# A hybrid decoder block: a bank of its own for retention's state, weight differences kept between two stages, and eight pages for the x sums

## The chip, the core and the metric

The kernel runs on one core of a Trainium2 chip. The metric is the device time of one execution in microseconds, lower is better. The core's engines are TensorE (PE in the profile, its weight loads PEld), VectorE (DVE), ScalarE (ACT), GpSimd (POOL) and SyncE (SP), whose queue issues nearly all DMAs of the part that this case is about. Each engine takes its instructions in the order in which the program gives them to it. Matmuls write to PSUM, which the kernel uses as eight banks, each 128 partitions x 512 fp32.

## The reference

One decoder layer on x of 1024 tokens x 1024 channels, in float32:

```
h    = rms_norm(x)
P    = h @ w_in                       # retention q, k, v, gate: 4 x 512; attention: the rest
ret  = retention, 8 heads of 64 channels, chunks of 128 tokens:
         inner = (q k^T) * decay mask
         o     = inner @ v + (q * decay) @ state
         state = state * decay + (k * decay)^T @ v
ret  = rms_norm per head(ret) * silu(gate)
dif  = differential attention, 4 heads (two softmax maps per head)
x    = x + concat(ret, dif) @ w_out
x    = x + (silu(h2 @ w_gate) * (h2 @ w_up)) @ w_down,   h2 = rms_norm(x), 2816 wide
```

## The kernel before

**Products.** Every fp32 operand is split into a high part and the rest, both fp32r, and a term of a matrix product is three matmuls (high x high, rest x high, high x rest). The input projection of retention's columns is made by seven products in the place of eight (Strassen's way), once for each half p of the columns: p = 0 runs P2, P4, P6, P7, P5, P3 (its P1 and half of P2 stand beside the last attention units, in `lead`), p = 1 runs P1, P2, P6, P5, P3, P7, P4. A product is four tiles j = 0 to 3 of 128 tokens x 512 columns; a tile adds four inner blocks k into one bank, so it is 4 x 3 = 12 matmuls. It needs its weights, four pages of 128x512 (k = 0 to 3) that `prepare` makes out of blocks of w_in and splits (`halves_`: ACT writes the high part `whi`, DVE the rest `wlo`), and its x block. For P6, P7, P5 and P3 this is a sum of blocks of the normalised x that was written to memory earlier (`sumd`): `x_sum` loads one page, ACT casts the high part and DVE subtracts the rest. The pages for these loads are the two `raw` pages, in turn.

**P6, P4 of the first half.** Four weight blocks a, b, d, c of each k go into P4, P6, P5, P3 and P7. Beside the last attention units (steps ND to ND + 2 of the first loop) `t4_load`, `t4_minus`, `t4_scale` and `t4_sum` load them, make the differences a - b and d - c, and of these the weights of P4 into pages named `spare` (and `pr[8]`); the table `EARLY` says which pages. P6 of p = 0 then loads a, b and c of each k again, subtracts a - b again, and makes its weights of that; P5, P3 and P7 use the a and c pages of P6.

**Retention.** A unit (p, t) is a group p of four heads and a chunk t of 128 tokens, t in order. Its steps: load and rotate q and k (DVE); turn, four transposes on PE, copied out of the bank by ACT; inner, q k^T into bank 6; DVE multiplies by the mask into `iT`; state, (k)^T v into columns 256 to 511 of bank 7, which DVE adds to the running state `rg`, GpSimd scaling it; out, iT v and q state into columns 0 to 255 of bank 7; ACT copies it out and squares it, DVE reduces, GpSimd takes the reciprocal root, ACT scales, DVE multiplies by the gate. `mix_turn(t)` transposes what the units of chunk t left and splits it for `o_proj`, the product with w_out; `norm` transposes its result for the FFN. The transposes of the units go through bank 3, those of `mix_turn` and `norm` through banks 1 and 2.

**Order.** From the second product stage on to the first FFN products, each step is a job with an engine, an estimated duration, and keys that it reads and writes (`add`). `Plan` sets one time for every job: products have goals in their order, other jobs a latest time worked back from these, and a list schedule with the estimated durations gives the order on every engine; PE's own order is made this way too. A key stands for a buffer: two jobs are ordered only where a key is shared. The two halves of bank 7 have keys of their own, `b7o` (out) and `b7u` (state).

In the rows below, `h`, `m` and `pp` are PSUM tiles; `h_4014` is bank 6, `h_4015` bank 7, `m_4011` bank 3, `pp_3703` and `m_4010` banks 1 and 2. `wx` and `wy` are the two big pages that hold retention's small tiles (rotated q and k, iT, v, gates, state), `rowa_89` to `rowa_96` the pages `mixd[0]` to `mixd[7]`, `spare_3700` the eight spare pages, `cd` the memory that holds partial sums.

Of the kernel before, what the change touches and what calls it, by code (L numbers as in the profile page):

```python
# [107 lines left out]
def block_kernel(ctx: ExitStack, tc: tile.TileContext, x, norm1_g, w_in, ret_norm_g, dq_g, dk_g,  # L108
# [508 lines left out]
    def t4_load(k, which=range(4)):  # L617
        early[k] = [spare[at] for at in EARLY[k]]
        for n in which:
            SY.dma_start(early[k][n].rearrange("p (a b) -> p a b", b=256), win_block(0, n % 2, n // 2 * 4 + k))  # L620
# [8 lines left out]
    def t4_sum(k):  # L629
        a, b, d, c = early[k]  # L630
        V.scalar_tensor_tensor(out=d, in0=d, scalar=g1col[:, 4 + k:5 + k], in1=b, op0=ALU.mult, op1=ALU.subtract)

    EARLY = [(0, 1, 2, 3), (4, 5, 6, 7), (0, 1, 3, 4), (5, 7, 8, 4)]
    LEAD = {ND: [(4, snap, 0), (1, t4_load, 0), (2, t4_load, 1), (5, t4_minus, 0, 0), (7, t4_minus, 0, 1)],
            ND + 1: [(0, snap, 1), (4, c11, 0), (0, t4_scale, 0), (1, t4_minus, 1, 0), (2, t4_sum, 0), (3, t4_load, 2, range(3)),
                     (4, t4_minus, 1, 1), (5, t4_scale, 1), (6, t4_sum, 1),
                     (6, t4_load, 2, (3,)), (7, t4_load, 3, range(3))],
            ND + 2: [(0, c11, 1), (4, snap, 2), (0, t4_minus, 2, 0), (1, t4_minus, 2, 1), (2, t4_load, 3, (3,)),
                     (2, t4_scale, 2), (3, t4_minus, 3, 0), (4, t4_sum, 2), (5, t4_scale, 3), (6, t4_minus, 3, 1),
# [6 lines left out]
    for s in range(ND + 3):  # L646
        if s == ND:
            difw.close()
            prp = ctx.enter_context(tc.tile_pool(name="prp", bufs=9, side="right"))
            pr = [prp.tile([P, 512], F32, tag="pr", name="pr") for _ in range(9)]  # L650
            late["spare"] = act.tile([P, 8 * 512], F32, tag="act", name="spare")
            spare += [late["spare"][:, i * 512:(i + 1) * 512] for i in range(8)] + [pr[8]]
            small = prp.tile([P, 48], F32, name="small", bufs=1)
            lead_bank += [bankp(), bankp()]
            main = lead()
            order["pinned"] = True
            r_tables()
            order["pinned"] = False
# [23 lines left out]
    sx = ctx.enter_context(tc.tile_pool(name="sx", bufs=3))  # L682
    sxt = [sx.tile([P, 4, 2, 4, P], F32R, tag="sx", name="sx") for _ in range(3)]
    sbs = ExitStack()
# [109 lines left out]
    def dma(to, src, r=(), w=(), **kw):  # L794
        return add("SP", 0.8, lambda: SY.dma_start(to, src), r, w, lag=2.8, **kw)

# [30 lines left out]

    spare = [(f"R{i}", page) for i, page in enumerate(spare[:8])]
    prk = [(f"pr{i}", pr[i]) for i in range(9)]
    rowk = [(f"ra{i}", mixd[i]) for i in range(NT)]  # L830
    rawk = [(f"raw{i}", wp.tile([P, 512], F32, tag="raw", name="raw", bufs=NRAW)) for i in range(2)]
    held = [spare[2], spare[6], spare[3], prk[8]]
    wraw = Ring(rowk[4:8] + [prk[8]])
    keep_r = Ring([spare[i] for i in (0, 4, 5, 7, 1, 2, 6, 3)])
    sraw = Ring(rawk)
# [25 lines left out]
    def prepare(p, name, k, n):  # L861
# [4 lines left out]
        elif name == "P6":  # L866
            a, c = keep_r(), keep_r()
            held_w[k] = a, c
            (ka, a), (kc, c) = a, c
            load_raw(ka, a, p, 0, 0, k)  # L870
            kb, b = rawload(p, 0, 1, k)
            load_raw(kc, c, p, 1, 1, k)
            tt(a, a, b, ALU.subtract, [ka, kb], [ka])
            act_copy(b, a, [ka], [kb], ga)
# [26 lines left out]
    def x_sum(name, j):  # L901
        key, page = sraw()
        dma(page, sumd[SUM_OF[name], j], (), [key])
        hi, lo = (BLOCK[name][:, j, i].rearrange("p k e -> p (k e)") for i in range(2))
        act_copy(hi, page, [key], [f"x{name}{j}h"])
        tt(lo, page, hi.bitcast(F32), ALU.subtract, [key, f"x{name}{j}h"], [f"x{name}{j}l"])

# [100 lines left out]
    ca_r, cb_r = Ring(rowk[0:2]), Ring(rowk[2:4])  # L1008
    turn_bank, side_bank = Ring([3]), Ring([1, 2])
    WS = ["rc", "rn", "sqr", "onr", "qkr0", "qkr1", "qkr2", "qbd0", "qbd1", "vh0", "vh1", "gs0", "gs1",  # L1010
# [6 lines left out]
    def unit(p, t, due=None):  # L1017
# [45 lines left out]
        if t + 1 < NT:  # L1063
            def state():
                for a in range(2):
                    T.matmul(bank[7][:, 256 + a * P:256 + (a + 1) * P], qkr[:, 256 + a * P:256 + (a + 1) * P],
                             vh[:, a * P:(a + 1) * P], start=True, stop=True)
            add("PE", 0.46, state, [qk, vk], ["b7u"])
            gg = cs[:, C_G128 + 2 * p:C_G128 + 2 * p + 2].unsqueeze(2)
            up = bank[7][:, 256:512].rearrange("p (a e) -> p a e", e=P)  # L1070
            o_, n_ = (x_[1].rearrange("p (a e) -> p a e", e=P) for x_ in (old, new))
            for hd in range(2):
                h = halves[hd]
                if t > 0:
                    tt(n_[h, :, h], up[h, :, h], o_[h, :, h], ALU.add, ["b7u", old[0]], [new[0]], dur=0.3)
                else:
                    tt(n_[h, :, h], up[h, :, h], gg[h].broadcast_to([HD, 2, HD]), ALU.mult, ["b7u"], [new[0]], dur=0.3)
            if t > 0:
                tt(n_, n_, gg.broadcast_to([P, 2, P]), ALU.mult, [new[0]], [new[0]], "POOL", 1.1)

        def out_():
            for a in range(2):
# [3 lines left out]
                for hd in range(2):  # L1086
                    T.matmul(o[:, hd * HD:(hd + 1) * HD], iT[:, (2 * a + hd) * P:(2 * a + hd + 1) * P],
                             vh[:, a * P + hd * HD:a * P + (hd + 1) * HD], start=t == 0, stop=t == 0 or hd == 1)
        add("PE", 1.37 if t else 0.92, out_, [tk, ik, vk] + ([old[0]] if t else []), ["b7o"])
        stay = p == 0 and t < 4  # L1090
        mk, m_ = onr if stay else prk[4 + t % 4]
        ob = m_ if stay else m_[:, 256 * p:256 * p + 256]
        add("ACT", 0.28, lambda: A.copy(ob, bank[7][:, 0:256]), ["b7o"], [mk])
        sq4 = sqr[1].rearrange("p (g d) -> p g d", d=HD)
# [64 lines left out]
    def mix_turn(t):  # L1159
        key, page = px[t][1]  # L1160
        dma(page, mixdd[t], (), [key])
        for q, (key, page) in enumerate((prk[4 + t % 4], px[t][1])):
            b = side_bank()

            def go(b=b, page=page):
                for j in range(4):
                    T.transpose(bank[b][:, j * P:(j + 1) * P], page[:, j * P:(j + 1) * P], ident)
            add("PE", 0.36, go, [key], [f"b{b}"])
            n = 2 * (t % 2) + q
            hi, lo = slot[n]  # L1170
            act_copy(hi, bank[b], [f"b{b}"], [f"wh{n}"], dur=0.48)
            tt(lo, bank[b], hi.bitcast(F32), ALU.subtract, [f"b{b}", f"wh{n}"], [f"wl{n}"])
# [41 lines left out]
    def norm(t):  # L1214
# [11 lines left out]
        for q in (t // 4, 1 - t // 4):  # L1226
# [362 lines left out]
```

## Time and profile before

| | |
|---|---|
| median of 3 runs | 1200.89 us (1200.55 to 1201.44) |
| the profiled execution | 1201.5 us, of which the span of instructions is 1199.7 us |
| granted clock of TensorE | 1.00 |
| busy: PE, DVE, ACT, POOL | 1182.1, 911.8, 607.1, 528.4 us |

The stages by the trace, in us from the start of the span:

| stretch | what runs | PE busy |
|---|---|---|
| 0 to 273.10 | attention, its projection, P1 and P2 of p = 0 | 265.72 of 273.10 |
| 273.10 to 332.22 | P4, P6, P7, P5, P3 of p = 0 | 57.29 of 59.12 |
| 332.22 to 436 | the seven products of p = 1, first units | 103.78 of 103.78 |
| 436 to 486 | o_proj, most units | 46.47 of 50.00 |
| 486 to 571 | o_proj, norm | 85.00 of 85.00 |
| 571 to 600 | first FFN products | 28.17 of 29.00 |
| 600 to 1199 | FFN | 595.70 of 599.00 |

A row of the trace gives the start in us, the length in us, the engine, line and operation with out<-in, and in brackets how long the engine was idle just before and what released it. All operations are recorded by one helper, so their line is L136 everywhere. A matmul on fp32 operands (retention's) counts as two. A row of waits gives what waited <- what it waited for: us in total, times, the longest. A row of groups gives a kind of instruction, xcount, then busy us, mean ns | idle time before them and its releasers. A row of the chain (the work that ended last, followed back) has start, length and what ran.

### The profile page before, as it was taken

The numbers are of one execution on the slowest core, as the hardware profiler recorded it, in microseconds if no ns is written. First come the engines' busy times: TensorE is split into PE (matmuls) and PEld (weight loads), VectorE is DVE, ScalarE is ACT, GpSimd is POOL, SyncE is SP. The second block draws the span as 40 slices with busy tenths as digits, with TensorE's granted clock in tenths as the row PEclk, the third lists the DMA queues.
The fourth block names the chain that finished last, engine by engine and source line by source line (L and its number), as shares of the span: only waits on it lengthen the run. The fifth ranks groups of instructions, "written<-read, shape, count | busy, mean of one in ns | idle before, by whom it ended". The sixth has DMA issues, their size and how long they took to land.

```text
span 1199.7 us, 17494 instructions
## 1 busy us (share of the span) xinstructions
PE 1182.1 (99%) x5872; PEld 1000.7 (83%) x5872; DVE 911.8 (76%) x1533; ACT 607.1 (51%) x1332; POOL 528.4 (44%) x611
## 2 busy tenths in 40 slices
PE   8999999999999999999999999999999999999998
PEld 6898989887788887888888888888888888888887
DVE  6987888887878978547988666666666659798696
ACT  6865666656365758635544434343443434444442
POOL 2678787630001214211077545654466536164053
PEclk9999999999999999999999999999999999999999
DMA  7267676358844754222233233323234277933341
GB/s 207 67 138 144 97 137 105 80 185 263 292 150 152 254 170 141 90 78 71 89 114 124 96 100 111 115 98 96 93 109 132 74 266 266 377 106 97 97 128 73
DMA packets 120984, 167.42 MB, mean 140 GB/s; under 512 B 12096, under 2 KB 65472, under 8 KB 120768
## 3 DMA queue, kind: packets, MB, share of 16 engines
q1 hardware_dynamic: 113952, 155.76, 40.1%
q0 software_dynamic: 5760, 10.49, 6.7%
q8 instruction: 46, 0.75, 0.3%
q14 instruction: 42, 0.34, 0.1%
q10 hardware_dynamic: 1184, 0.07, 0.1%
HBM read 114.12 MB, written 54.26 MB: 140 GB/s over the span
## 4 chain that ended last, share of the span: by engine, by line
PE 89%; DVE 5%; DMA 3%; ACT 2%; issue 1%; POOL 0%; SPq 0%; DVEq 0%; ACTq 0%
PE h L136 39%; PE pp L136 29%; PE m L136 19%; PE big L136 3%; DMA raw<-sumd 1%; DVE wlo L136 1%; DVE pr L136 1%; DMA spare<-in_w_in_dram 1%; DVE wx L136 1%; DMA more<-in_w_in_dram 0%; DMA rowa<-in_w_in_dram 0%; DVE wy L136 0%; DVE q L136 0%; ACT whi L136 0%; DVE sx L136 0%
## 5 line engine op out<-in xcount | busy, mean ns | idle before, releaser
L136 POOL TENSOR_TENSOR sum<-rawp 128x512 f32<-128x512 f32 x100 | 142.5, 1427 | 174.2 <-DVE wlo L136 141.3
L136 ACT CAST whi<-sum 128x512 fp32r<-128x512 f32 x155 | 96.4, 622 | 200.8 <-POOL sum L136 65.4
L136 PE MATMUL pp<-whi,act 128*128 128x384 f32 (+1 forms) x624 | 191.2, 357 | 1.3 <-ACT whi L136 0.8
L136 DVE TENSOR_TENSOR wlo<-sum,whi 128x512 fp32r<-128x512 f32 x155 | 158.5, 1023 | 35.1 <-ACT whi L136 34.9
L136 POOL TENSOR_TENSOR sum<-wide 128x512 f32<-128x512 f32 x55 | 86.4, 1571 | 128.4 <-DVE wlo L136 99.6
L136 PEld LDWEIGHTS pp<-whi,act 128*128 128x128 f32 x624 | 115.5, 188 | 6.3 <-ACT whi L136 1.0
L136 PE MATMUL h<-sx,whi 128*128 128x512 f32 x360 | 112.0, 392 | 0.0
L136 PE MATMUL pp<-wlo,act 128*128 128x384 f32 (+1 forms) x312 | 108.2, 347 | 0.6 <-DVE wlo L136 0.6
L136 DVE TENSOR_TENSOR wlo<-wide,whi 128x512 fp32r<-128x512 f32 x99 | 79.7, 828 | 31.6 <-ACT whi L136 31.6
L136 ACT CAST whi<-wide 128x512 fp32r<-128x512 f32 x99 | 59.4, 621 | 83.0 <-PE m L136 43.2
L136 PEld LDWEIGHTS h<-sx,whi 128*128 128x128 f32 x360 | 66.9, 188 | 13.3
L136 DVE TENSOR_TENSOR wlo<-rawp,whi 128x512 fp32r<-128x512 f32 x44 | 47.2, 1073 | 39.3 <-ACT whi L136 38.5
L136 PE MATMUL h<-whi 128*128 128x512 f32 x196 | 77.0, 393 | 0.0
L136 PE MATMUL h<-whi,wlo 128*128 128x512 f32 x196 | 76.3, 390 | 0.0
L136 PE MATMUL h<-wlo,whi 128*128 128x512 f32 x196 | 76.3, 389 | 0.0
L136 DVE TENSOR_TENSOR c<-c,h 128x512 f32<-128x512 f32 x80 | 52.9, 682 | 30.5 <-PE h L136 30.5
L136 POOL TENSOR_TENSOR fsum<-c 128x512 f32<-128x512 f32 x50 | 71.1, 1431 | 8.5 <-DMA ffd<-fsum 8.5
L136 PE MATMUL h<-sx,wlo 128*128 128x512 f32 x180 | 70.2, 390 | 0.0
L136 PEld LDWEIGHTS pp<-wlo,act 128*128 128x128 f32 x312 | 58.9, 189 | 3.6 <-DVE wlo L136 1.2
L136 PE MATMUL h<-b,whi 128*128 128x512 f32 x176 | 54.4, 390 | 0.0
L136 ACT CAST whi<-rawp 128x512 fp32r<-128x512 f32 x44 | 27.3, 620 | 47.1 <-PE h L136 17.5
L136 ACT ACTIVATE p<-big,nm 128x128 f32<-128x128 f32 (+7 forms) x64 | 47.6, 744 | 6.0 <-DVE nm L136 5.3
(310 smaller groups left out, 3161.3 us busy)
## 6 DMA issues: line engine op xcount, KB each, us to landing
wide<-ffd SPq DMA_DIRECT2D x77, 256.0 KB, 2.7
ffd<-fsum SPq DMA_DIRECT2D x55, 256.0 KB, 2.0
rawp<-in_w_gate_dram SPq DMA_DIRECT2D x22, 512.0 KB, 3.8
rawp<-in_w_up_dram SPq DMA_DIRECT2D x22, 512.0 KB, 3.8
wide<-in_w_down_dram SPq DMA_DIRECT2D x44, 256.0 KB, 5.4
sumd<-act POOLq DMA_DIRECT2D x40, 256.0 KB, 5.6
rowa<-cd SPq DMA_DIRECT2D x32, 256.0 KB, 3.2
spare<-in_w_in_dram SPq DMA_DIRECT2D x31, 256.0 KB, 4.6
```

What stands on the lines that cost most here:

```text
L136: i = getattr(self.engine, op)(*(now(a) for a in args), **{k: now(a) for k, a in kw.items()})
```

## The change

- State goes to columns 0 to 255 of bank 3 (key `b3`), out stays in bank 7 (key `b7`); `bank_keys` follows. The units' turns go to banks 1 and 2, from one ring with the transposes of `mix_turn`.
- `t4_load` takes other pages: a and c in two spare pages for each k, d in `mixd[k]`, b in spare 6, spare 7, `pr[8]`, `pr[7]`. The table `EARLY` goes; the loads for k = 2 and 3 stand earlier in `LEAD`. a - b and c then stay, and P6 of p = 0 takes them: 12 loads of 256 KB and 4 subtractions on DVE are not made. P4 takes its weights from `mixd[0]` to `mixd[3]`.
- The x sums of P6, P7 and P5 are loaded into a ring of eight pages `xraw`, in the third `sx` slot. P3's block, which had that slot from the start, is opened when the last of the eight has been read (`open_sx2`, key `sx2`); P3's sums still come through the two `raw` pages.
- The estimates of the plan are 0.85 in the place of 0.8 us for a DMA and 0.45 in the place of 0.36 for the transposes of `mix_turn` and `norm`.

```diff
     def t4_load(k, which=range(4)):
-        early[k] = [spare[at] for at in EARLY[k]]
+        early[k] = [spare[2 * k], (spare[6], spare[7], pr[8], pr[7])[k], mixd[k], spare[2 * k + 1]]
...
-            ND + 1: [(0, snap, 1), (4, c11, 0), (0, t4_scale, 0), (1, t4_minus, 1, 0), (2, t4_sum, 0), (3, t4_load, 2, range(3)),
+            ND + 1: [(0, snap, 1), (4, c11, 0), (0, t4_scale, 0), (1, t4_minus, 1, 0), (2, t4_sum, 0), (0, t4_load, 2),
...
-                     (6, t4_load, 2, (3,)), (7, t4_load, 3, range(3))],
+                     (3, t4_load, 3, (0, 1, 2)), (7, t4_load, 3, (3,))],
...
-    sxt = [sx.tile([P, 4, 2, 4, P], F32R, tag="sx", name="sx") for _ in range(3)]
+    sxt = [sx.tile([P, 4, 2, 4, P], F32R, tag="sx", name="sx") for _ in range(2)]
+    xraw_t = sx.tile([P, 8 * 512], F32, tag="sx", name="xraw")
...
+    xraw = Ring([(f"xr{i}", xraw_t[:, i * 512:(i + 1) * 512]) for i in range(8)])
+
+    def open_sx2():
+        late["sx2"] = sx.tile([P, 4, 2, 4, P], F32R, tag="sx", name="sx")
+
+    sxt.append(lazy("sx2"))
...
-    held = [spare[2], spare[6], spare[3], prk[8]]
+    held = rowk[0:4]
     wraw = Ring(rowk[4:8] + [prk[8]])
-    keep_r = Ring([spare[i] for i in (0, 4, 5, 7, 1, 2, 6, 3)])
...
         elif name == "P6":
-            a, c = keep_r(), keep_r()
-            held_w[k] = a, c
-            (ka, a), (kc, c) = a, c
-            load_raw(ka, a, p, 0, 0, k)
-            kb, b = rawload(p, 0, 1, k)
-            load_raw(kc, c, p, 1, 1, k)
-            tt(a, a, b, ALU.subtract, [ka, kb], [ka])
+            (ka, a), (kc, c) = held_w[k] = spare[2 * k], spare[2 * k + 1]
+            if p:
+                load_raw(ka, a, p, 0, 0, k)
+                kb, b = rawload(p, 0, 1, k)
+                load_raw(kc, c, p, 1, 1, k)
+                tt(a, a, b, ALU.subtract, [ka, kb], [ka])
+            else:
+                kb, b = wraw()
             act_copy(b, a, [ka], [kb], ga)
...
     def x_sum(name, j):
...
-        key, page = sraw()
+        key, page = sraw() if name == "P3" else xraw()
+        if name == "P3" and j == 0:
+            add("NONE", 0.0, open_sx2, (), [k_ for k_, _ in xraw.items] + ["sx2"])
         dma(page, sumd[SUM_OF[name], j], (), [key])
...
-    turn_bank, side_bank = Ring([3]), Ring([1, 2])
+    turn_bank = side_bank = Ring([1, 2])
...
-                    T.matmul(bank[7][:, 256 + a * P:256 + (a + 1) * P], qkr[:, 256 + a * P:256 + (a + 1) * P],
+                    T.matmul(bank[3][:, a * P:(a + 1) * P], qkr[:, 256 + a * P:256 + (a + 1) * P],
                              vh[:, a * P:(a + 1) * P], start=True, stop=True)
-            add("PE", 0.46, state, [qk, vk], ["b7u"])
+            add("PE", 0.46, state, [qk, vk], ["b3"])
...
-            up = bank[7][:, 256:512].rearrange("p (a e) -> p a e", e=P)
+            up = bank[3][:, 0:256].rearrange("p (a e) -> p a e", e=P)
...
-        add("PE", 1.37 if t else 0.92, out_, [tk, ik, vk] + ([old[0]] if t else []), ["b7o"])
+        add("PE", 1.37 if t else 0.92, out_, [tk, ik, vk] + ([old[0]] if t else []), ["b7"])
...
-        return ["b7o", "b7u"] if b == 7 else [f"b{b}"]
+        return [f"b{b}"]
```

The order that the plan makes of it moves at three places. First, SP's queue at the start of P4 of p = 0, before the change: loads of w_in for P6 (`spare`, `rowa_93` to `rowa_96`), with the first pages of `sumd` between them.

```order
L136 DMA spare_3700<-in_w_in_dram 128x2x256
L136 DMA rowa_95<-in_w_in_dram 128x2x256
L136 DMA spare_3700<-in_w_in_dram 128x2x256 x2
L136 DMA rowa_96<-in_w_in_dram 128x2x256
L136 DMA spare_3700<-in_w_in_dram 128x2x256
L136 DMA raw_4016<-sumd_196 128x512
L136 DMA spare_3700<-in_w_in_dram 128x2x256 x2
L136 DMA raw_4017<-sumd_196 128x512
L136 DMA pr_3699<-in_w_in_dram 128x2x256
L136 DMA cd_197<-pr_3697 128x512
```

The same place after the change:

```order
L136 DMA cd_197<-pr_3696 128x512
L136 DMA mixdd_199<-rowa_95 128x512
L136 DMA xraw_4002<-sumd_196 128x512
L136 DMA mixdd_199<-rowa_96 128x512
L136 DMA xraw_4002<-sumd_196 128x512 x2
L136 DMA pr_3699<-in_w_in_dram 128x2x256
L136 DMA xraw_4002<-sumd_196 128x512 x5
L136 DMA cd_197<-pr_3697 128x512
L136 DMA raw_4016<-sumd_196 128x512
L136 DMA raw_4017<-sumd_196 128x512
```

The loads of w_in are gone, and the pages of `sumd` go out one after the other; `mixdd` and `cd` are stores.

Second, PE's queue around state of unit (1, 3), before the change. The rows are inner (1, 3), the turn of unit (0, 4), state (1, 3), three matmuls of o_proj, out (1, 3), inner (0, 4), the turn of (1, 4), state (0, 4).

```order
L136 MATMUL h_4014<-wx_4637,wy_4638 128x256 x2
L136 MATMUL m_4011<-cs_77,wx_4637 128x128 x4
L136 MATMUL h_4015<-wy_4638,wx_4637 128x128 x2
L136 MATMUL h_4013<-sx_4002,whi_3063 128x512 x2
L136 MATMUL h_4013<-sx_4002,wlo_3064 128x512
L136 MATMUL h_4015<-wy_4638 128x128
L136 MATMUL h_4015<-wy_4638 128x64 x2
L136 MATMUL h_4015<-wy_4638 128x128
L136 MATMUL h_4015<-wy_4638 128x64 x2
L136 MATMUL h_4014<-wx_4637,wy_4638 128x256 x2
L136 MATMUL m_4011<-cs_77,wx_4637 128x128 x4
L136 MATMUL h_4015<-wy_4638,wx_4637 128x128 x2
```

After the change the same state stands inside P4 of p = 1, among the transposes of `mix_turn` (`pr_3697`, `rowa_95`), out (1, 3) standing nine matmuls and two transpose groups before it, and the next step of a unit, state (0, 4), following after six more matmuls and one transpose group.

```order
L136 MATMUL h_4012<-whi_3375,act_88 128x512
L136 MATMUL h_4012<-wlo_3376,act_88 128x512
L136 MATMUL h_4012<-whi_3375,act_88 128x512
L136 MATMUL pp_3703<-cs_77,pr_3697 128x128 x4
L136 MATMUL m_4011<-wy_4623,wx_4622 128x128 x2
L136 MATMUL m_4010<-cs_77,rowa_95 128x128 x4
L136 MATMUL h_4012<-whi_3478,act_88 128x512
L136 MATMUL h_4012<-wlo_3479,act_88 128x512
L136 MATMUL h_4012<-whi_3478,act_88 128x512
L136 MATMUL h_4013<-whi_3178,act_88 128x512
```

State (1, 3) has moved ahead of about 25 groups of three matmuls, out of o_proj into the projection.

Third, PE's queue after the change where units 4 and 5 now stand, late in o_proj: inner (1, 4), three matmuls, the turn of (0, 6), three matmuls, out (1, 4), inner (0, 5), state (0, 5). In the queue before, the turn of (1, 4) and the steps of (0, 4) are the rows shown above for it.

```order
L136 MATMUL h_4014<-wx_4622,wy_4623 128x256 x2
L136 MATMUL pp_3702<-sx_4232,whi_3063 128x512 x2
L136 MATMUL pp_3702<-sx_4232,wlo_3064 128x512
L136 MATMUL pp_3703<-cs_77,wx_4622 128x128 x4
L136 MATMUL pp_3702<-sx_4232,whi_3063 128x512 x2
L136 MATMUL pp_3702<-sx_4232,wlo_3064 128x512
L136 MATMUL h_4015<-wy_4623 128x128
L136 MATMUL h_4015<-wy_4623 128x64 x2
L136 MATMUL h_4015<-wy_4623 128x128
L136 MATMUL h_4015<-wy_4623 128x64 x2
L136 MATMUL h_4014<-wx_4622,wy_4623 128x256 x2
L136 MATMUL m_4011<-wy_4623,wx_4622 128x128 x2
```

No state shares a bank with an out any more, and two groups of three matmuls and a turn stand between this inner and its out; nearly all steps of units 4 to 7 stand beside tiles 2 and 3 of o_proj, where they stood beside tiles 0 to 2 before.

More of the change, by code (lines that the diff above doesn't have):

```diff
@@ L631, in t4_sum @@
         V.scalar_tensor_tensor(out=d, in0=d, scalar=g1col[:, 4 + k:5 + k], in1=b, op0=ALU.mult, op1=ALU.subtract)
-    EARLY = [(0, 1, 2, 3), (4, 5, 6, 7), (0, 1, 3, 4), (5, 7, 8, 4)]
     LEAD = {ND: [(4, snap, 0), (1, t4_load, 0), (2, t4_load, 1), (5, t4_minus, 0, 0), (7, t4_minus, 0, 1)],
-            ND + 1: [(0, snap, 1), (4, c11, 0), (0, t4_scale, 0), (1, t4_minus, 1, 0), (2, t4_sum, 0), (3, t4_load, 2, range(3)),
+            ND + 1: [(0, snap, 1), (4, c11, 0), (0, t4_scale, 0), (1, t4_minus, 1, 0), (2, t4_sum, 0), (0, t4_load, 2),
                      (4, t4_minus, 1, 1), (5, t4_scale, 1), (6, t4_sum, 1),
-                     (6, t4_load, 2, (3,)), (7, t4_load, 3, range(3))],
-            ND + 2: [(0, c11, 1), (4, snap, 2), (0, t4_minus, 2, 0), (1, t4_minus, 2, 1), (2, t4_load, 3, (3,)),
+                     (3, t4_load, 3, (0, 1, 2)), (7, t4_load, 3, (3,))],
+            ND + 2: [(0, c11, 1), (4, snap, 2), (0, t4_minus, 2, 0), (1, t4_minus, 2, 1),
                      (2, t4_scale, 2), (3, t4_minus, 3, 0), (4, t4_sum, 2), (5, t4_scale, 3), (6, t4_minus, 3, 1),
@@ L651, in block_kernel @@
             late["spare"] = act.tile([P, 8 * 512], F32, tag="act", name="spare")
-            spare += [late["spare"][:, i * 512:(i + 1) * 512] for i in range(8)] + [pr[8]]
+            spare += [late["spare"][:, i * 512:(i + 1) * 512] for i in range(8)]
             small = prp.tile([P, 48], F32, name="small", bufs=1)
@@ L794, in dma @@
     def dma(to, src, r=(), w=(), **kw):
-        return add("SP", 0.8, lambda: SY.dma_start(to, src), r, w, lag=2.8, **kw)
+        return add("SP", 0.85, lambda: SY.dma_start(to, src), r, w, lag=2.8, **kw)
     def act_copy(to, src, r, w, scale=None, dur=0.53, **kw):
@@ L901, in x_sum @@
     def x_sum(name, j):
-        key, page = sraw()
+        hi, lo = (BLOCK[name][:, j, i].rearrange("p k e -> p (k e)") for i in range(2))
+        hk, lk = f"x{name}{j}h", f"x{name}{j}l"
+        key, page = sraw() if name == "P3" else xraw()
+        if name == "P3" and j == 0:
+            add("NONE", 0.0, open_sx2, (), [k_ for k_, _ in xraw.items] + ["sx2"])
         dma(page, sumd[SUM_OF[name], j], (), [key])
-        hi, lo = (BLOCK[name][:, j, i].rearrange("p k e -> p (k e)") for i in range(2))
-        act_copy(hi, page, [key], [f"x{name}{j}h"])
-        tt(lo, page, hi.bitcast(F32), ALU.subtract, [key, f"x{name}{j}h"], [f"x{name}{j}l"])
+        act_copy(hi, page, [key, "sx2"] if name == "P3" else [key], [hk])
+        tt(lo, page, hi.bitcast(F32), ALU.subtract, [key, hk], [lk])
     MM3 = 0.681
@@ L1074, in unit @@
                 if t > 0:
-                    tt(n_[h, :, h], up[h, :, h], o_[h, :, h], ALU.add, ["b7u", old[0]], [new[0]], dur=0.3)
+                    tt(n_[h, :, h], up[h, :, h], o_[h, :, h], ALU.add, ["b3", old[0]], [new[0]], dur=0.3)
                 else:
-                    tt(n_[h, :, h], up[h, :, h], gg[h].broadcast_to([HD, 2, HD]), ALU.mult, ["b7u"], [new[0]], dur=0.3)
+                    tt(n_[h, :, h], up[h, :, h], gg[h].broadcast_to([HD, 2, HD]), ALU.mult, ["b3"], [new[0]], dur=0.3)
             if t > 0:
@@ L1092, in unit @@
         ob = m_ if stay else m_[:, 256 * p:256 * p + 256]
-        add("ACT", 0.28, lambda: A.copy(ob, bank[7][:, 0:256]), ["b7o"], [mk])
+        add("ACT", 0.28, lambda: A.copy(ob, bank[7][:, 0:256]), ["b7"], [mk])
         sq4 = sqr[1].rearrange("p (g d) -> p g d", d=HD)
@@ L1167, in go @@
                     T.transpose(bank[b][:, j * P:(j + 1) * P], page[:, j * P:(j + 1) * P], ident)
-            add("PE", 0.36, go, [key], [f"b{b}"])
+            add("PE", 0.45, go, [key], [f"b{b}"])
             n = 2 * (t % 2) + q
@@ L1236, in go @@
                     T.transpose(bank[b][:, j * P:(j + 1) * P], page[:, j * P:(j + 1) * P], ident)
-            add("PE", 0.36, go, [key], bks)
+            add("PE", 0.45, go, [key], bks)
             if q == t // 4:
```

## The prediction

> **What bounds the kernel now.** I read the page first, then busy time by stage, then the waits of PE stage by stage, and last the rows around each wait.
>
> ```profile
> span 1199.7 us, 17494 instructions
> PE 1182.1 (99%) x5872; PEld 1000.7 (83%) x5872; DVE 911.8 (76%) x1533; ACT 607.1 (51%) x1332; POOL 528.4 (44%) x611
> ...
> 273.10:332.22 59.12, 57.29 (x241) 44.11 (x240) 48.04 (x76) 30.50 (x51) 0.00 (x0) 1.00 0.88 284
> 332.22:436.00 103.78, 103.78 (x521) 87.56 (x520) 86.78 (x152) 65.44 (x148) 14.09 (x21) 1.00 0.59 192
> 436.00:486.00 50.00, 46.47 (x299) 39.92 (x298) 38.69 (x82) 39.00 (x123) 18.29 (x29) 1.00 0.38 116
> 486.00:571.00 85.00, 85.00 (x431) 71.06 (x431) 49.59 (x79) 42.03 (x98) 11.96 (x25) 1.00 0.26 83
> 571.00:600.00 29.00, 28.17 (x142) 24.04 (x141) 28.12 (x48) 15.53 (x28) 1.84 (x2) 1.00 0.26 86
> 600.00:1199.00 599.00, 595.70 (x2628) 492.73 (x2626) 434.97 (x552) 240.82 (x416) 304.55 (x209) 1.00 0.41 134
> ```
>
> The columns of the windows are length, then busy us (xinstructions) of PE, PEld, DVE, ACT, POOL, the clock, the DMA share, GB/s. TensorE is busy 99% of the span, so a gain is only what its waits leave, unless matmuls go, and the count of jobs on PE doesn't change. The change touches the windows up to 600. In them PE idles 1.83 us between 273 and 332, 3.53 between 436 and 486, 0.83 after 571, and not at all in the other two.
>
> In the first window idle time is not the whole loss, since a stopped PE also restarts slowly. A better yardstick is the length of a product's tile where nothing stops it:
>
> ```profile
> 326.88 5.51 PE h L136 x24
> 332.39 2.72 PE pp L136 x12
> ```
>
> A tile of 12 matmuls takes 2.72 to 2.76 us. P4 to P3 of p = 0 are 20 tiles, 54.4 to 55.1 us, and take 59.12. So 4.0 to 4.7 us are lost there, 1.83 as idle time and the rest in restarts.
>
> What ends the waits there:
>
> ```profile
> L136 ACT CAST sx<-raw 128x512 fp32r<-128x512 f32 x12 | 7.4, 618 | 18.9 <-DMA raw<-sumd 18.7
> L136 DVE TENSOR_TENSOR sx<-raw,sx 128x512 fp32r<-128x512 f32 x12 | 8.2, 687 | 5.2 <-ACT sx L136 5.2
> L136 ACT ACTIVATE rowa<-spare,g1col 128x512 f32<-128x512 f32 x7 | 5.1, 722 | 8.8 <-DVE spare L136 8.8
> L136 DVE SCALAR_TENSOR_TENSOR rowa<-spare,g1col,rowa 128x512 f32<-128x512 f32 x4 | 3.0, 750 | 0.2
> L136 DVE TENSOR_TENSOR spare<-spare,rowa 128x512 f32<-128x512 f32 x4 | 2.8, 693 | 4.5 <-DMA rowa<-in_w_in_dram 4.5
> ...
> 272.56 4.82 DMA rowa<-in_w_in_dram
> 277.39 6.38 DMA spare<-in_w_in_dram
> ...
> 299.27 4.19 DMA raw<-sumd
> 303.48 0.63 ACT sx L136
> ...
> 286.47 0.50 PE L136 MATMUL h<-wlo,sb 128*128 128x512 f32 x1 [0.53 <-DVE wlo L136]
> ...
> 324.30 0.73 PE L136 MATMUL pp<-whi,sx 128*128 128x512 f32 x2 [0.56 <-DVE sx L136]
> ```
>
> The first five rows are groups between 268 and 330. ACT stands 18.7 us waiting for pages of x sums: with two pages in turn, a load starts only when DVE has read the page two before, and takes 3.4 to 4.8 us to land. P6 waits for its weights, whose raw blocks land only 10 us after their loads began (272.56 to 283.77), and P5 and P3 wait for x sums.
>
> In the second window, with the rows of the two other engines between those of PE:
>
> ```profile
> PE h L136 <- DVE wy L136: 2.4, 4, 0.7
> PE h L136 <- ACT pr L136: 1.1, 3, 0.6
> ...
> 444.13 0.37 ACT L136 COPY pr<-h 128x256 f32<-128x256 f32 x1 [2.27 <-DVE wy L136]
> 444.56 0.71 PE L136 MATMUL h<-wy,wx 128*128 128x128 f32 x4 [0.19 <-ACT pr L136]
> ...
> 446.15 0.69 DVE L136 TENSOR_TENSOR wy<-h,cs 128x512 f32<-128x512 f32 x1
> 446.90 0.55 PE L136 MATMUL h<-wy 128*128 128x64 f32 x3 [0.71 <-DVE wy L136]
> ...
> 455.86 0.37 ACT L136 COPY pr<-h 128x256 f32<-128x256 f32 x1
> 456.29 0.71 PE L136 MATMUL h<-wy,wx 128*128 128x128 f32 x4 [0.58 <-ACT pr L136]
> ...
> 474.90 0.29 DVE L136 TENSOR_TENSOR wy<-h,wy 64x128 f32<-64x128 f32 x1
> 475.34 0.63 PE L136 MATMUL h<-wy 128*128 128x128 f32 x4 [0.67 <-DVE wy L136]
> ```
>
> Seven waits, 3.5 us. Two kinds are to be told apart. At 444.56 and 456.29 a state starts right after ACT has copied out of the other half of bank 7, which state neither reads nor writes; at 475.34 an out starts right after DVE has added from the state half. The keys of the plan don't order these; something in the program or the chip orders them by bank. These three are 0.19 + 0.58 + 0.67 = 1.44 us. The other kind is at 446.90: out waits for the mask product `iT`, which is late because DVE is behind.
>
> **The change, part by part.**
>
> *x sums and early differences, 273 to 332.* The 12 loads for P6 (3 MB beside 12 pages of sums) and 4 DVE subtractions of 693 ns go; the differences are in place before. So each of P6's four weight pages needs ACT's scaling (0.72), one DVE operation (0.75) and the split (0.62 on ACT, 0.69 on DVE), and each of its four x pages a split. That is 12 operations on either engine, some 8 to 9 us from 273.6 on, with P4's evictions between them: ready by about 282 to 283, against a need at 284.0 (four tiles after 273.1) and the 286.47 of now. The x sums of P6, P7, P5 go out in a row of eight from about 271, when the last attention pages are free. At 4 to 5 us for the first and 0.92 us from page to page (256 KB at this window's mean 284 GB/s), P6's four land by about 279, the eighth by 283. After that ACT and DVE, 0.62 and 0.69 us a page, set the pace and not a page's round trip: I work out P7 ready near 291 (needed 295), P5 near 297 (needed 306), P3 near 309 (needed 316). DVE, 48.04 us busy in 59.12, loses 2.8 and would hold 45.2 of 55, so it is what comes next, but not full. The term: −4.3 us, near the whole loss since each step has 1 to 8 us of margin; bounds −4.7 and 0 (the waits come back as waits for DVE).
>
> P3's block is opened only after the eight pages are read. That holds ACT's P3 casts until the last P5 page is read, near 297, and P3's loads stand behind it on `raw`, 88 and 89 in SP's rows; two more follow at 3.4 to 4.8 us each. Margin 7 us: nothing. On SP the sums stand ahead of the store `mixdd<-rowa_96` and of one weight load; SP is in order, and what waits behind the first sum waits for the release of attention's pages, as the loads of w_in did before. Nothing. The earlier loads of k = 2, 3 in `LEAD` stand beside products that don't wait on PE: nothing.
>
> *State in a bank of its own.* The three waits by bank go, 1.44 us of idle time. Beside them DVE's additions no longer wait until out leaves bank 7: by the rows of groups, `wy<-h,wy` (state's additions) stand idle 5.4 us for PE in this stretch:
>
> ```profile
> L136 DVE TENSOR_TENSOR wy<-h,wy 64x128 f32<-64x128 f32 x18 | 5.2, 288 | 7.3 <-PE h L136 5.4 <-ACT pr L136 1.8
> ```
>
> So DVE is less late for `iT`. Also the order moves: units to (1, 3) are done before P4 ends, where DVE has room, and units 4 to 7 stand beside later tiles, with two or one groups between inner and out (the rows of the order). A group of three matmuls is 0.68 us (a quarter of 2.72), a turn about 0.45, a state 0.46: the cover of inner (1, 4) in the rows of the order is 1.8 us, that of inner (1, 3) before was 1.6. These are the shortest of each; a mask takes 0.69, and its queue on DVE decides. I take the three waits as gone, each with an estimated 0.15 us of restart (the first window shows more, 2.2 us or more beyond the idle time of its waits): 1.9, and of the remaining 2.1 us a third: together −2.6. Bounds: −4.6 (all seven with restarts) and 0 (each wait finds a new place).
>
> The Trainium skill's page "PSUM — Partial Sum Buffer", section "PSUM bank collisions raise a hardware error", says that software must order any two engines on one bank and quadrant even for different columns, and that the compiler's scheduler adds such an order. The rows at 444.56, 456.29 and 475.34 agree. By the plan's keys, which treat halves as apart, the bank move itself would be worth 0 and this term only what reordering gives, −0.7, for 1195.9; by the page it is the −1.9 that I use.
>
> *Shared turn banks.* Turns of units now share banks 1 and 2 with `mix_turn` and `norm`, so a turn can wait for an eviction of another kind.
>
> ```profile
> L136 ACT COPY wx<-m 64x256 f32<-64x256 f32 x20 | 7.3, 363 | 2.5 <-PE m L136 2.2
> L136 ACT COPY wy<-m 128x512 f32<-128x512 f32 x10 | 5.8, 578 | 0.0
> ```
>
> A turn's evictions are three ACT copies, 0.58 and 2 x 0.36 us, and the order leaves about 3 us of PE's work or more between two uses of a bank: 0, bounds 0 and +1, for one or two uses that find ACT behind.
>
> *Later.* At 571 a wait of 0.83 for the last `norm`; its distance hardly changes: 0, bounds −0.9 and +0.5.
>
> ```profile
> 573.02 0.62 PE L136 MATMUL pp<-act,whi 128*128 128x384 f32 x2 [0.83 <-DVE b L136]
> ```
>
> From 600 on, 595.70 of 599 busy and the same order: nothing.
>
> Sum against the profiled execution, 1201.5 us (span 1199.7 and 1.8 around it): 1201.5 − 4.3 − 2.6 = 1194.6. The median of the runs, 1200.89, is 0.6 lower, so 1194.0.
>
> **The rivals.**
>
> *One: retention's stalls move.* Units 4 to 7 now stand in 20 groups of three matmuls, denser than before; DVE, at 38.69 of 50 us, makes `iT` late in new places. For it: four of the seven waits are for DVE now. Against: its waits on bank 7 go. Then only the first term pays: 1196.6.
>
> *Two: the sums come no earlier.* SP issues in order and the first `xraw` load waits for attention's pages; if these are free only at 280, P6 waits as now and only P5's and P3's waits go. For it: the DMA share is 0.88 in this window. Against: half of P6's bytes are gone. Then −1.5 to −2 with the second term: 1196.7 to 1198; with both rivals, no change.
>
> *Three, slower: `mix_turn` waits for crowded units.* Units (1, 0) to (1, 3) now end within some 15 us, and `mix_turn(0)` to `(2)` stand in P4 of p = 1, about 9, 10 and 11 us of PE's work after the out that they need. How long a unit takes from out to its last product with the gate:
>
> ```profile
> 371.01 1.00 PE L136 MATMUL h<-wy 128*128 128x64 f32 x8
> 376.35 0.42 DVE L136 TENSOR_TENSOR wy<-wx,wy 128x256 f32<-128x256 f32 x1
> ...
> 442.18 0.83 PE L136 MATMUL h<-wy 128*128 128x128 f32 x6
> 454.65 0.42 DVE L136 TENSOR_TENSOR pr<-pr,wy 128x256 f32<-128x256 f32 x1
> ```
>
> 4.8 us where units stand alone (372.01 to 376.77), 12.1 us in the crowd (out ends 443.01, the product 455.07). At 12.1 the first `mix_turn` waits about 3 us, and as PE is in order the others then find theirs done: 1197 if the rest holds. It decides for slower by over 0.2% only from a wait of 9.3 us (the gains of 6.9 and 2.4 more), a unit of some 18 us, longer than any seen.
>
> **How the numbers follow.** A difference under 0.2%, 2.4 us, can't be told from none. The forecast, both terms near their size, 1194.0: 0.58. Its own range, 1191.5 (both terms full, the wait at 571 gone) to 1196. Retention's stalls move, 1196.6: 0.20. Sums no earlier, 1197.5: 0.08, of which 0.02 with no change at all. `mix_turn` waits: 0.09, of which 0.03 far enough to be slower and 0.03 within 0.2%. The rest, 0.05, for a wait not seen here: 0.03 slower, 0.02 same. Of the first rival 0.03 lies within 0.2%, where the first term is halved too. So faster 0.84, same 0.02 + 0.03 + 0.02 + 0.03 = 0.10, slower 0.03 + 0.03 = 0.06. The range 1190.8 to 1197.8 takes in the full terms below and the first two rivals above.
>
> **What would show it.** Right: ACT's wait for pages of sums falls from 18.7 to a few us; PE's rows of P4 to P3 fall from 59.1 to about 55; no state or out of retention starts behind a read of another tile's bank; waits in o_proj under 2 us. Wrong: PE waits for `rowa` or `pr` at the transposes of `mix_turn` in P4 of p = 1; waits for `sx` from DVE while its pages have landed (DVE the bound); a row of waits at inner or out between 470 and 510.

## The result and the profile after

The changed kernel takes 1190.84 us (median of 6 runs, 1190.46 to 1192.11) against 1200.73 for the kernel before in the same comparison: a ratio of 0.9918, 95% interval 0.9905 to 0.9931, 9.9 us faster. The profiled execution took 1190.47 us, its span 1188.7.

First the page of the changed kernel, then its busy time by stretches cut at the same places of the program as before: P4 to P3 of p = 0; from P1 of p = 1 to the first FFN product; the first FFN products.

```profile
span 1188.7 us, 17471 instructions
PE 1178.3 (99%) x5872; PEld 1002.3 (84%) x5872; DVE 908.9 (76%) x1529; ACT 605.4 (51%) x1332; POOL 527.4 (44%) x611
```
```profile
272.78:327.18 54.40, 54.40 (x242) 45.05 (x240) 46.20 (x73) 27.84 (x48) 0.00 (x0) 1.00 0.76 248
327.18:553.02 225.84, 225.75 (x1205) 191.73 (x1204) 165.48 (x299) 138.05 (x355) 43.40 (x72) 1.00 0.46 143
553.02:593.92 40.90, 40.52 (x202) 34.58 (x201) 40.60 (x69) 24.93 (x46) 4.88 (x5) 1.00 0.23 72
```

The second stretch of the kernel before:

```profile
332.22:563.45 231.23, 227.70 (x1210) 192.08 (x1208) 167.97 (x301) 140.26 (x356) 43.14 (x72) 1.00 0.44 140
```

The first stretch is 54.40 us, exactly 20 tiles of 2.72, where it was 59.12: 4.7 us less. The second is 225.84 where it was 231.23: 5.4 us less, of which idle time is 3.4 (3.53 before, 0.09 after) and 2.0 is busy time. About 0.4 of the 2.0 is work that only moved over the cut: four transposes of `norm` (563.09 to 563.45 before) stand ahead of the first FFN product there and behind it in the changed kernel, so at equal work the second stretch is 5.0 us shorter. The rest of the busy time is taken up further down. What is left of the 11.0 us between the two spans is spread: 0.3 before P4, 0.1 in the first FFN products (0.5 at equal work), 0.4 behind.

All that PE waits for from 274 us to the end of the FFN, in the changed kernel, and the groups of ACT and DVE that answer to those shown of before (the x sums between 268 and 326, state's additions between 425 and 486):

```profile
PE pp L136 <- DVE b L136: 0.4, 1, 0.4
```
```profile
L136 ACT CAST sx<-xraw 128x512 fp32r<-128x512 f32 x8 | 4.6, 618 | 0.0
L136 ACT CAST sx<-raw 128x512 fp32r<-128x512 f32 x4 | 2.5, 618 | 9.3 <-DMA raw<-sumd 5.7 <-issue 3.5
```
```profile
L136 DVE TENSOR_TENSOR wy<-m,wy 64x128 f32<-64x128 f32 x10 | 2.9, 287 | 1.1 <-PE m L136 0.9
```

One wait of PE is left of the thirteen that were there between 273 and 573. ACT's waits for pages of sums are down from 18.7 us to 5.7, all at P3's pages, and state's additions hardly wait: over the whole second stretch all 24 of them stand idle 1.4 us, where they stood 7.6 before.

### The profile page after: what moved, and what is told of

It reads as the page before. It is cut to its first block, busy times and chain, and to the rows that moved or that the text cites. A ratio compares the mean times of both kernels' runs of the same rounds, so it can differ in the third digit from the quotient of the medians.

```text
span 1188.7 us, 17471 instructions
## 1 busy us (share of the span) xinstructions
PE 1178.3 (99%) x5872; PEld 1002.3 (84%) x5872; DVE 908.9 (76%) x1529; ACT 605.4 (51%) x1332; POOL 527.4 (44%) x611
## 4 chain that ended last, share of the span: by engine, by line
PE 93%; DVE 4%; ACT 1%; issue 1%; POOL 1%; DMA 0%; SPq 0%; DVEq 0%; ACTq 0%
PE h L136 40%; PE pp L136 31%; PE m L136 19%; PE big L136 3%; DVE wlo L136 1%; DMA more<-in_w_in_dram 0%; POOL small L136 0%; DVE wy L136 0%; DVE q L136 0%; DVE wx L136 0%; ACT wx L136 0%; ACT whi L136 0%; DVE p L136 0%; DVE pr L136 0%; DVE acc L136 0%
## 5 line engine op out<-in xcount | busy, mean ns | idle before, releaser
L136 DVE TENSOR_TENSOR wlo<-rawp,whi 128x512 fp32r<-128x512 f32 x44 | 49.9, 1133 | 38.8 <-ACT whi L136 37.8
L136 DVE TENSOR_REDUCE nm<-big 128x1 f32<-128x128 f32 (+7 forms) x64 | 48.5, 758 | 2.2
```

The source lines that it names most:

```text
L136: i = getattr(self.engine, op)(*(now(a) for a in args), **{k: now(a) for k, a in kw.items()})
```

## The experiments

Two questions: which of the parts pays where, and by what. The table gives each run's ratio to the kernel before with its 95% interval, and from its trace the length of the 20 tiles (start of P4 to start of P1, 54.40 if nothing waits) and of the stretch from there to the first FFN product. Each ratio is against runs of the kernel before that were taken with that kernel; their medians were 1200.73, 1200.0, 1199.8 and 1200.8 us. In the changed kernel and in those made of it with the new estimates, the last column is 0.4 us shorter by the four transposes alone.

| kernel | median us | ratio | 20 tiles | P1 to FFN |
|---|---|---|---|---|
| before | 1200.73 | 1 | 59.12 | 231.23 |
| changed | 1190.84 | 0.9918 [0.9905, 0.9931] | 54.40 | 225.84 |
| bank alone | 1194.0 | 0.9949 [0.9936, 0.9963] | 56.81 | 226.20 |
| pages and differences | 1197.07 | 0.9975 [0.9965, 0.9985] | 54.40 | 231.31 |
| differences alone | 1196.46 | 0.9973 [0.9961, 0.9984] | 54.40 | 231.24 |
| pages alone | 1198.08 | 0.9986 [0.9977, 0.9994] | 54.61 | 231.30 |
| changed, state in bank 7 | 1195.05 | 0.9956 [0.9942, 0.9969] | 54.40 | 229.16 |
| changed, old estimates | 1191.78 | 0.9932 [0.9919, 0.9944] | 54.40 | 225.53 |
| changed, four pages | 1191.29 | 0.9930 [0.9916, 0.9944] | 54.40 | 226.05 |
| changed, two pages | 1191.15 | 0.9928 [0.9914, 0.9941] | 54.40 | 226.10 |
| changed, no pages | 1191.09 | 0.9923 [0.9910, 0.9937] | 54.40 | 225.80 |
| changed, no pages, two copies more | 1191.71 | 0.9927 [0.9911, 0.9942] | 54.40 | 226.64 |
| changed, two copies more | 1191.49 | 0.9926 [0.9910, 0.9943] | 54.40 | 226.88 |
| before, two early loads | 1198.31 | 0.9984 [0.9975, 0.9993] | 55.13 | 231.29 |

### The parts one by one

**The bank alone:** in the kernel before, state in bank 3 and the ring [1, 2] for turns and side transposes.

```diff
-    turn_bank, side_bank = Ring([3]), Ring([1, 2])
+    turn_bank = side_bank = Ring([1, 2])
...
-                    T.matmul(bank[7][:, 256 + a * P:256 + (a + 1) * P], ...
+                    T.matmul(bank[3][:, a * P:(a + 1) * P], ...
```

> Before, with the state's own bank and the shared turn banks alone. Theory 'the parts add up, each in its own stage': the stretch from P1 of p = 1 to the end of o_proj shortens by about 5.0 us as in the changed kernel, the loss of 4.0 to 4.7 us between 273 and 332 stays; in all 1195.0 to 1196.5. Rival 'the order needs all parts': the gain after 332 came from an order of jobs that the pages helped to make; the bank alone gives 2 us or less, 1198.5 or more.

Measured: 0.9949, 6.1 us, to 1194.0, 1 us below the range of the theory; the second stretch takes 226.20 us, 5.0 less than before. The rival falls: the bank and the order that follows from it pay alone. What PE waits for in its trace after 327 us:

```profile
PE pp L136 <- DVE b L136: 0.8, 1, 0.8
PE h L136 <- ACT wx L136: 0.6, 1, 0.6
PE m L136 <- DVE wlo L136: 0.2, 1, 0.2
```

None of the seven waits on `wy` and `pr` is left. The 0.6 is new: an inner waits for ACT's copy of its turn.

What was not expected: its 20 tiles take 56.81 us, 2.3 less than before, though the instructions of these tiles are the same in the same order. The difference comes in from outside. In the profiled execution of before, two operations of GpSimd on one column took half a microsecond longer each than in the profile of the bank alone. First before, then the bank alone:

```profile
267.99 0.77 POOL L136 TENSOR_SCALAR mo<-so,epso 128x1 f32<-128x1 f32 x1 [3.79 <-ACT sqo L136]
268.85 1.07 POOL L136 TENSOR_TENSOR ro<-mo,cs 128x1 f32<-128x1 f32 x1
```
```profile
267.76 0.27 POOL L136 TENSOR_SCALAR mo<-so,epso 128x1 f32<-128x1 f32 x1 [3.77 <-ACT sqo L136]
268.11 0.57 POOL L136 TENSOR_TENSOR ro<-mo,cs 128x1 f32<-128x1 f32 x1
```

They stand in the chain to the store that SP waits for before P6's loads. So that store went out 1.05 us later in that execution (270.66 against 269.61), the loads behind it too, and PE lost 4.7 us and not 2.4. That the one follows from the other is read from the rows; no run isolates it. The profiled execution of before, 1201.5 us, lies 0.7 to 1.7 us above the medians of before, so its profile overstates this term: by up to 2.3 us against this other execution, by less against a usual one.

**Pages and differences, without the bank:** the other edits, with the old estimates.

> Before, with the eight pages and the kept differences, without the bank. Theory 'the parts add up': the 20 tiles from P4 to P3 of p = 0 take 54.4 to 54.6 us in the place of 59.1, the seven waits of o_proj stay at about 3.5 us; in all 1195.8 to 1196.4. Rival 'the order needs all parts': the waits of o_proj change by more than 1.5 us, either way.

Measured: 54.40 us for the 20 tiles, and the waits of o_proj as before, to the tenth:

```profile
PE h L136 <- DVE wy L136: 2.4, 4, 0.7
PE h L136 <- ACT pr L136: 1.1, 3, 0.6
```

The gains of the two halves, 6.1 and 3.0 us, add up to 9.1, against 9.9 of the change, within the intervals. The time, 1197.07, is 0.7 us above the range that was expected. A part is the reason just given: 4.7 us was to be won by the tiles of one execution, and 3.0 was won by the medians. In this run's trace P4 also starts at 274.23, 1.1 us later than before; with the differences alone it starts at 273.05, and whether the delay belongs to the change isn't shown.

**The differences alone, and the pages alone.** The edits to `t4_load`, `LEAD`, `held` and P6; then the edits to `sxt`, `xraw` and `x_sum`, with P6 loading and subtracting as before.

> Before, with the kept differences alone (12 loads and 4 subtractions less, two pages for the x sums). Theory 'loads': the waits of P6 go (1.7 us by the starts of the tiles), and with 12 loads fewer on the queue the pages of sums land sooner, so that of the 3.0 us of P5 and P3 a half goes too: 1197 to 1199. Rival 'the ring': two pages in turn set the pace whatever the queue holds; ACT's wait for pages stays over 15 us and only P6's share goes, 1198.8 to 1199.3.

> Before, with the eight pages alone (P6 loads and subtracts as before). Theory 'loads': the eight loads of sums now stand among the 12 loads of P6 and make them later; P6 waits as long or longer (1.7 us or more), P5 and P3 wait no more: 1197.5 to 1198.5. Rival 'the ring': the two pages were the whole trouble, P6's x too; P6's wait halves and the rest goes: 1196.5 to 1197.2.

Measured: in the 20 tiles both went better than either theory allowed. With the differences alone, and two pages, they take 54.40 us, with the pages alone 54.61. So in these traces each of the two does the whole work. By the medians the differences alone gain 3.2 us (0.9973) and both together 3.0 (0.9975), so the pages add nothing measurable to the differences. The pages alone gain 1.7 (0.9986; their 1198.08 us lies in the range of 'loads'), and the intervals don't tell whether that is less. What ACT waits for in the run with the differences alone, between 268 and 325:

```profile
ACT sx L136 <- DMA raw<-sumd: 14.1, 6, 3.7
```

ACT waits for pages of sums as long as before (14.6 in the same window), and PE waits for nothing. This wait, which I had read as what ends PE's waits, is slack: PE loses nothing by it. In every run with two pages here ACT waits for pages; whether PE does too depends on how far ahead the pages run.

### Does the ring need eight pages?

The ring of eight cut to four and to two pages, then taken out (`sxt` with three blocks, x sums through `raw`).

```diff
-    xraw = Ring([(f"xr{i}", xraw_t[:, i * 512:(i + 1) * 512]) for i in range(8)])
+    xraw = Ring([(f"xr{i}", xraw_t[:, i * 512:(i + 1) * 512]) for i in range(4)])
```

> The changed kernel with four pages of the ring of eight. Theory 'loads': with P6's loads gone a page comes back in 5 to 6 us (load 4, ACT and DVE 1.3), four in flight give one every 1.4 us, while a product of four tiles needs four in 10.9 us, so four pages are enough: within 0.5 us of the changed kernel. Rival 'the ring': a wait of over 0.5 us for sums returns at P6 or P5, 1191.5 or more.

> The changed kernel with two pages of the ring of eight (beside the two raw pages that P3 has for itself). Theory 'loads': a page every 2.7 us at best, enough for P7 and P5 at 2.72 us a tile but not for P6, whose four pages must be there when P4 ends; 1 to 2 us lost: 1192 to 1193. Rival 'the ring': as before the change, 3 to 4.7 us lost, 1193.8 to 1195.5.

> The changed kernel without the eight pages: bank, kept differences and new estimates, x sums through the two raw pages as before. Theory 'head start': what the pages must have is an early first load; without P6's 12 loads ahead of it the first sum goes out near 269.5 and two pages, at one page in 2.7 to 3 us, keep 20 tiles at 54.4 to 54.6 us; in all 1190 to 1191.6, the changed kernel's time. Rival 'the pages pay their share': 0.5 to 3 us lost between 273 and 332, 1191.5 to 1194.

Measured: 54.40 us in all three, and 1191.1 to 1191.3 us. I expected two pages to cost 1 to 2 us; they cost nothing. The kernel without the ring is the changed kernel's equal within what can be told. In its trace, the two stretches:

```profile
272.74:327.14 54.40, 54.40 (x242) 45.07 (x240) 46.02 (x72) 27.94 (x47) 0.00 (x0) 1.00 0.76 241
327.14:552.94 225.80, 225.71 (x1206) 191.81 (x1204) 166.32 (x300) 138.45 (x356) 43.90 (x72) 1.00 0.45 143
```

### What made the pages late

Three runs on why two pages were too few before and are enough now. In the first, the kernel without the ring gets two more ACT copies that write the two `raw` pages from P4's first tile, so that the first loads of sums can't go earlier than in the kernel before; in the second the changed kernel gets the same on two of its eight pages. In the third, the kernel before issues its first two loads of sums ahead of P6's weights (at 232.49 and 240.01, long before P4 starts); nothing else of it is touched.

```diff
             if name == "P4":
                 act_copy(d, m, [bk], [dk], dur=0.48)
+                if j == 0:
+                    for key, page in rawk:
+                        act_copy(page, m, [bk], [key], dur=0.48)
```
```diff
-        dma(page, sumd[SUM_OF[name], j], (), [key])
+        if (name, j) in (("P6", 0), ("P6", 1)) and not early_x.get(j):
+            early_x[j] = True
+            SY.dma_start(page, sumd[SUM_OF[name], j])
+        else:
+            dma(page, sumd[SUM_OF[name], j], (), [key])
```

> The kernel of the run before it (no eight pages), with two copies more on ACT that write the two raw pages from the first tile of P4, and so hold back the first two loads of x sums until about 276.5 to 277, where the kernel before had them; no loads for P6. Theory 'head start': the loss of before returns without any of P6's loads: 20 tiles take 57 to 59.5 us, with waits at P6, P5 and P3; 2.5 to 5 us over the run before it. Rival 'loads': without 3 MB beside them the pages come back faster and catch up; under 1.5 us lost, all at P6.

> The changed kernel with the same two copies into the first two of the eight pages, so that its first load of x sums is also held back to about 276.5 to 277. Theory 'head start': P6 waits as in the run before it (0.5 to 2 us), but eight pages let the later loads run ahead, so that P7, P5 and P3 wait for nothing: 54.9 to 56.4 us for the 20 tiles. Rival 'ACT and DVE set the pace': after the late start P5 and P3 wait too, 57 us or more.

> Before, with only the first two loads of x sums (P6, tiles 0 and 1) issued ahead of all of P6's weight loads; two pages, all 12 loads and 4 subtractions stay. Theory 'head start': the third and fourth page start some 8 us earlier than before, and the waits of P5 and P3 go (3 us) while P6 still waits for its weights (0.5 to 1.5): 20 tiles in 54.9 to 56.3 us, 1197 to 1198.5 in all. Rival 'loads': with the queue as full as before the pages come back as slowly, P5 and P3 wait 2 us or more: 57.5 us or more.

Measured: my theory of the head start falls as it was put, and its rival 'loads' has the time right. With the first load held back to 276.62 PE still waits for nothing: 54.40 us of PE work in 54.40 (by the traces this run differs from the kernel without the ring by one later wait of an inner for ACT, 0.8 us). ACT waits for pages even longer than before, at no loss:

```profile
ACT sx L136 <- DMA raw<-sumd: 21.1, 9, 4.5
```

With eight pages PE waits for nothing either, but there the plan let the other six pages go ahead of the two that were held, from 269.83, so that run doesn't test a late start. What differs from before is how long the first page took. Issue and first read of a page, before and then with the two copies:

```profile
276.72 0.34 SPq L136 DMA_DIRECT2D raw<-sumd  x1
283.53 0.62 ACT L136 CAST sb<-raw 128x512 fp32r<-128x512 f32 x1
285.18 0.32 SPq L136 DMA_DIRECT2D raw<-sumd  x1
```
```profile
276.62 0.32 SPq L136 DMA_DIRECT2D raw<-sumd  x1
279.67 0.64 ACT L136 CAST sb<-raw 128x512 fp32r<-128x512 f32 x1
281.07 0.34 SPq L136 DMA_DIRECT2D raw<-sumd  x1
```

Both issue the first load at the same time. Before, it goes out behind ten of P6's twelve loads, takes 6.3 us to land and is read 6.8 us after its issue; without them it lands in 2.7 us and is read after 3.1. So the third load, which must wait for that page, goes at 285.18 and not at 281.07. The kernels with two pages and all of P6's loads fall in line: the third load goes at 285.18 in before and 4.7 us are lost, at 283.57 in the bank alone and 2.4 are lost, at 278.94 with two early loads and 0.7 are lost (P4 starts at 273.10, 272.86 and 274.02). First the bank alone, then the two early loads:

```profile
283.57 0.32 SPq L136 DMA_DIRECT2D raw<-sumd  x1
272.86:329.67 56.81, 56.17 (x241) 44.58 (x240) 47.88 (x76) 30.57 (x51) 0.00 (x0) 1.00 0.89 291
```
```profile
278.94 0.34 SPq L136 DMA_DIRECT2D raw<-sumd  x1
274.02:329.15 55.13, 54.83 (x241) 44.91 (x240) 46.19 (x73) 28.79 (x48) 0.00 (x0) 1.00 0.88 285
```
```profile
PE h L136 <- DVE wlo L136: 0.3, 1, 0.3
```

The 0.7 with two early loads are P6's own weights (`wlo`); P5 and P3 wait no more, at the same DMA share (0.88) and rate as before. That run speaks for the ring's start and against a mere want of bandwidth in P5 and P3. From the third load on, two pages turn over in about 2.9 us a page in before (the third at 285.18, the fifteenth at 320.55) and in the run with the two copies alike (281.07 to 315.83), just short of PE's 2.72 us a tile. So once P6's loads are through the two rings have one pace; without them the ring only starts 4.1 us earlier, and in before what is lost at the start is never won back.

### The bank or the order?

The changed kernel with state written to bank 7 again, under the plan's key of bank 3. The plan sees no difference, so all engines have the same instructions in the same order.

```diff
-                    T.matmul(bank[3][:, a * P:(a + 1) * P], ...
+                    T.matmul(bank[7][:, 256 + a * P:256 + (a + 1) * P], ...
-            up = bank[3][:, 0:256].rearrange("p (a e) -> p a e", e=P)
+            up = bank[7][:, 256:512].rearrange("p (a e) -> p a e", e=P)
```

> The changed kernel in its own order, state written to columns 256 to 511 of bank 7 again while the plan still takes it for bank 3 (bank 3 stays unused by it); every engine has the same instructions in the same order. Theory 'banks are ordered whole': the waits of a state for ACT's copy, of an out for DVE's additions and of DVE's additions for out come back, 1.5 to 4 us: 1192.4 to 1195. Rival 'the order did it': what shortened o_proj was where the units stand; PE waits under 0.5 us more, 1190.4 to 1191.5.

Measured: 1195.05 us; the second stretch takes 229.16, 3.3 us more than in the changed kernel. The stretch, PE's waits between 274 and 600, and the three largest in the rows of PE:

```profile
327.68:556.84 229.16, 226.85 (x1206) 191.14 (x1204) 165.82 (x299) 138.13 (x355) 43.61 (x72) 1.00 0.45 140
```
```profile
PE h L136 <- ACT pr L136: 1.2, 2, 1.1
PE h L136 <- DVE wy L136: 0.5, 1, 0.5
PE h L136 <- ACT wx L136: 0.5, 1, 0.5
PE pp L136 <- DVE b L136: 0.4, 1, 0.4
```
```profile
400.96 1.13 PE L136 MATMUL h<-wx,wy 128*128 128x256 f32 x4 [0.47 <-ACT wx L136]
404.85 1.10 PE L136 MATMUL h<-wy 128*128 128x64 f32 x8 [0.48 <-DVE wy L136]
494.05 0.71 PE L136 MATMUL h<-wy,wx 128*128 128x128 f32 x4 [1.07 <-ACT pr L136]
```

At 494.05 a state waits 1.07 us for ACT to copy out the other half of the bank, the wait of before in another place. The out at 404.85 waits for its mask product, with DVE behind. The inner at 400.96 waits for ACT's copies of its turn, and this wait comes and goes with the state in bank 3 too (0.2 us with two pages, 0.8 and 1.1 in the two runs with the copies), so up to 0.5 of the 3.3 us may not be the bank's. So 2.8 to 3.3 of the 5.4 us are the bank by itself, and about 2 are what the new order gives beside it, the 0.4 of the four transposes included. The waits stand in the program: several of DVE's additions from state carry a wait for ACT's semaphore there, and none does in the changed kernel. This is the order that the Trainium skill's page "PSUM — Partial Sum Buffer" states in "PSUM bank collisions raise a hardware error", for any two engines on one bank and quadrant, whichever columns they use; the run agrees with it, at 2.8 to 3.3 us.

**The estimates.** The changed kernel with 0.8 and 0.36 in the plan.

> The changed kernel with the plan's old estimates (0.8 for a DMA, 0.36 for the transposes). Theory 'the parts add up': the estimates only shift a few jobs; within 1 us of the changed kernel, 1190 to 1192. Rival 'the order is what pays': with the old estimates the units or the transposes stand where they wait, 2 us or more: 1193 or more.

Measured: 1191.78 us, and the wait of the first FFN products for the last `norm` is larger:

```profile
PE pp L136 <- DVE b L136: 0.8, 1, 0.8
```

It is 0.4 with the new estimates. By the traces the first FFN products take 41.61 us against 40.90, but the stretch ahead of them 225.53 against 225.84, with the four transposes in it; together 0.4 us more. The estimates thus give about 0.4 us there by the traces; in the medians (0.9 us) it can't be told from nothing. Nor is it firm: with the new estimates and two pages of the ring that wait is 0.7 us again.

## Why the prediction was right or wrong

The direction, the place of both gains and the range were right, the range by luck (1190.84, its lower end 1190.8; the forecast's own range ended at 1191.5): the sum −6.9 was 3.0 us short of −9.9.

- **x sums and differences, −4.3.** The trace shows −4.7, but the profile had caught before in an execution that lost 2.3 us more there than another; by medians the term is −3.0 (pages and differences together), so the good size is in part luck. Its cause was mis-split: I had both edits share the work, and by the tiles either alone does it. The step that failed is that a page's round trip sets the pace of two pages in turn and so makes PE wait: their pace was nearly enough, their late start was not, and two pages lose nothing in the changed kernel (54.40 us).
- **ACT's wait for pages,** named as a sign, fell from 18.7 to 5.7 as I said, and was worth nothing: 14.1 us of it stay without a loss in the run with the differences alone, 21.1 in the run with the two copies.
- **State in its own bank, −2.6.** The mis-sized term: −5.4 by the trace, −5.0 at equal work, beyond its bound of −4.6. "Of the remaining 2.1 us a third" was too little, all of them went; and the 0.45 us beyond idle time was about 1.6 at equal work, which the first window's ratio, 2.2 to 2.9 us beside 1.83 of idle time, had shown.
- **Shared turn banks, 0, bounds 0 and +1.** PE waits for no turn in the changed kernel. In its neighbours one wait of an inner for ACT's copies of a turn stands there, 0.2 to 1.1 us: the margin is thin.
- **Later, 0.** The wait at `norm` fell from 0.83 to 0.39 us. With the old estimates it is 0.8 again; I had not priced them.
- **The rivals.** Retention's stalls didn't move; the sums came earlier (the first load at 269.36); `mix_turn` waits for nothing, since PE has no such wait after 274 us. The estimate 1195.9 for a bank that orders nothing is refuted by the run with the old bank, 2.8 us at the least.

## What to carry to other kernels

A transfer ring whose pace is close to the consumer's, as the 2.9 us beside 2.72 here, is judged by where it starts: look at what stands ahead of its first pages in the DMA queues, and try taking that away before adding pages. An idle row with a large number ("waits for DMA 18.7 us") on an engine that isn't the bound is no price; the price is read at the bound, against a yardstick such as a stall-free tile. Two engines that used halves of one PSUM bank were ordered here as if they shared all of it, by waits that the planner's half-bank keys didn't show. So its keys should be banks, and a tensor that is read while its neighbour is written wants a bank to itself.

## What was not expected of the hardware

Two GpSimd operations on 128x1 took 0.77 and 1.07 us in one execution and 0.27 and 0.57 in another of the same code; the microsecond, on the way to a DMA queue, was followed by 2.3 us on TensorE. Why they were slow stays open. TensorE often lost more than its idle time: 4.7 us with 1.83 idle between 273 and 332. With the old bank, the same instructions in the same order have 2.2 us more idle time in the second stretch than in the changed kernel, and 1.1 more busy time. A part of this is how the rows are drawn: 128x512 matmuls start every 0.23 us and their rows are 0.39 long, so by estimate a gap of up to 0.16 us shows as no idle time; and the first row behind a wait can be 0.50 long (at 286.47 before). It isn't so for every wait: the inner's 0.84 us in the run with two copies and no ring lengthens the stretch by 0.84 (226.64 against 225.80).
